# One five-bank place for the scores of both softmax maps, three single banks for the rest, and the order of the attention written anew

## The chip, the core and the metric

The kernel runs on one core of a Trainium2 chip. TensorE (PE) multiplies matrices into PSUM, which has eight banks of 512 fp32 columns on 128 partitions; VectorE (DVE) and ScalarE (ACT) read PSUM and SBUF, GpSimd (POOL) reads SBUF alone, and SyncE (SP) issues the DMAs. Each engine works through its own list in order and waits on semaphores for the others. The metric is the time of one launch in microseconds; the median of three runs of the kernel before is 1440.42 us (1439.58 to 1440.72).

## The reference

Two layers over 1024 latent tokens and 128 prompt tokens, width 1024. Each layer normalizes and modulates the tokens (adaLN), projects them into q, k, v, gates and the inputs of two local branches, mixes by attention, Fourier and gMLP, projects back and normalizes. The part that the change touches is the differential attention: each of four heads has two maps of 64 dimensions, each with a softmax of its own, and the second is subtracted.

```python
def _diff_attention(q, k, v, lam, subln_w, lam_init):
    s = jnp.einsum('bhqmd,bhkmd->bhmqk', q, k,
                   preferred_element_type=jnp.float32) * (HEAD_DIM ** -0.5)
    p = jax.nn.softmax(s, axis=-1)
    a = p[:, :, 0] - lam * p[:, :, 1]
    o = jnp.einsum('bhqk,bhke->bhqe', a, v.astype(jnp.float32))
    o = (o * lax.rsqrt(jnp.mean(jnp.square(o), axis=-1, keepdims=True) + RMS_EPS)
         * subln_w.astype(jnp.float32) * (1.0 - lam_init))
    return o.astype(v.dtype)
```

The latent tokens attend to 1152 keys (1024 latent, rotated, and 128 cached); the prompt tokens attend to their own 128.

## The kernel before

All matmuls that carry precision are done with a number split in a high and a low part: `f32r` high parts, and the remainder as a second operand.

**Attention.** `attention` (L695) runs over 4 heads of 8 blocks of 128 queries, in each of the two layers: 64 blocks. A block's steps are: for each map m, `score` (L632) makes 128x1152 scores in a three-bank tile S by two passes of three 384-column matmuls (high q against K, then the remainder `qlo` padded with zeros to 128 rows); DVE takes the row maximum (`nm`, L640) and ACT the exponential with its row sum (`P`, L642). `softmax_diff` (L580) scales and subtracts the maps (POOL L584, DVE L585). One block later `transpose` (L646) turns the difference by nine transposes into one three-bank tile T, which ACT copies (L655) and DVE takes the remainder of (L656). For each two blocks, `values` (L658) multiplies with V in 27 matmuls into `pv`, and `finish_o` (L592) normalizes by a matmul with a constant matrix and a row of small ACT, POOL and DVE steps.

**PSUM before.** `psS` (L78) has two places of three banks; S, T, pv and the rest go through them in turn. `psM` (L81) has two single banks for projections (`z`, `zt`), V's transposes (`vt`) and the prompt's steps (`sp`, `atp`, `pvp`).

**Order.** PE's order is written by hand (`manual_schedule`, L1059): after each step `attention` yields, and `fill.fill` puts so much projection work (in nominal ns, `FILL` times `SHARE`) behind it. `fill.until` forces the units that a head needs before it starts. A second stream, `extra`, makes the modulation of the next layer (`mods`, L177: DVE multiply-adds named `macc`, then four matmuls `mres`) from head `MHEAD` on. A third, `side`, takes one step of the prompt's attention (`prompt`, L670) at a time. The other engines' order is made by a scheduler that goes by emission order with priorities.

After attention come the gMLP and Fourier branches (`local_gmlp`, `fourier_prepare`, `local_fourier`) and the output projection (`out_proj`), whose last steps make the next layer's input (`make_h`).

## Time and profile before

| | |
|---|---|
| profiled execution | 1439.59 us, of which the span from first to last instruction is 1437.7 us |
| PE | 1330.9 us busy (93%), 8264 matmuls |
| PE's weight loads | 1236.6 us (86%), beside the matmuls |
| DVE, ACT, POOL | 907.6 (63%), 746.6 (52%), 793.4 us (55%) |
| TensorE clock granted | 0.979 of full on the mean |
| DMA | 114.43 MB, mean 80 GB/s |

PE is busy almost throughout, and its records overlap: a matmul's row lasts from its start until its result is out, while the next one has started. The time that a matmul takes from the engine is the distance between two starts, which is got from a run of many. Idle time of PE, and what ended it, is in the list of waits; the profiled times of the first and last block's maxima place layer 0's attention at 97.7 to about 600 us and layer 1's at 808.4 to about 1275 us.

### The profile page before, as it was taken

The page shows a single profiled execution, that of the slowest core. Times are in us where ns is not written, and L with a number is a line of the kernel's source. Part 1 is how long each engine was busy: PE and PEld are TensorE (multiplying, and loading weights), DVE is VectorE, ACT ScalarE, POOL GpSimd, SP SyncE. Part 2 cuts the span into 40 slices and gives each one's busy share as a digit, 9 for nine tenths or more (in the row PEclk, how much of TensorE's full clock was granted, in tenths as well). Part 3 has the DMA queues.
Part 4 walks back from the last instruction along what each step waited for, and adds up shares of the span by engine and source line. Part 5 has one row for each costly group of instructions (what it writes and reads, how often), then busy time and mean ns, then how long its engine had stood idle before and what let it go on. Part 6 is the DMA issues. An engine that isn't in the chain of part 4 may idle for free. (4 is left out here: it accounts for less than half of the span.)

```text
span 1437.7 us, 21298 instructions
## 1 busy us (share of the span) xinstructions
PE 1330.9 (93%) x8264; PEld 1236.6 (86%) x8264; DVE 907.6 (63%) x1354; ACT 746.6 (52%) x1380; POOL 793.4 (55%) x723
## 2 busy tenths in 40 slices
PE   6899998889899999999997989989799999999997
PEld 4689998879788998987887989988789999998786
DVE  3646667787877865355785565668775684435576
ACT  3576666557454444353656565755565544435320
POOL 2455657567563446336687676575575343533752
PEclk9999999999999999999999999999999999999999
DMA  9310102211220221363341100112020010126432
GB/s 337 147 49 17 35 18 65 75 46 36 88 76 22 98 74 42 108 211 114 124 161 45 50 19 32 49 44 80 32 65 3 30 47 30 47 78 221 154 133 80
DMA packets 56158, 114.43 MB, mean 80 GB/s; under 512 B 4973, under 2 KB 32493, under 8 KB 55929
## 3 DMA queue, kind: packets, MB, share of 16 engines
q1 hardware_dynamic: 56056, 113.07, 23.7%
q8 instruction: 65, 1.06, 0.3%
q14 instruction: 37, 0.30, 0.1%
HBM read 95.47 MB, written 17.58 MB: 79 GB/s over the span
## 5 line engine op out<-in xcount | busy, mean ns | idle before, releaser
L386 PE MATMUL z<-H,w 128*128 128x384 f32 x2520 | 499.8, 345 | 22.4 <-DVE V L506 5.0
L386 PEld LDWEIGHTS z<-H,w 128*128 128x128 f32 x2520 | 444.9, 193 | 29.0 <-ACT vT L492 4.9
L642 ACT ACTIVATE P<-S,nm 128x1152 f32<-128x1152 f32 x128 | 156.4, 1222 | 118.6 <-DVE nm L640 112.1
L640 DVE TENSOR_REDUCE nm<-S 128x1 f32<-128x1152 f32 x128 | 172.3, 1349 | 40.4 <-PE S L638 39.9
L401 PE MATMUL zt<-whi,H 128*128 128x256 f32 x1152 | 158.7, 285 | 4.8 <-ACT ug L767 3.4
L401 PEld LDWEIGHTS zt<-whi,H 128*128 128x128 f32 x1152 | 147.0, 192 | 7.5 <-ACT ug L767 4.0
L584 POOL TENSOR_SCALAR P<-P,rz,neglam 128x1152 f32<-128x1152 f32 x64 | 86.8, 1356 | 98.3 <-DVE rz L583 87.2
L585 DVE SCALAR_TENSOR_TENSOR P<-P,rz 128x1152 f32<-128x1152 f32 x64 | 105.2, 1643 | 42.3 <-POOL P L584 42.3
L630 POOL TENSOR_TENSOR qlo<-qr,Q 64x128 fp32r<-64x128 f32 x128 | 81.4, 641 | 86.8 <-PE S L638 80.2
L367 POOL TENSOR_TENSOR w<-wraw,w 128x1024 fp32r<-128x1024 f32 x36 | 89.6, 2489 | 65.4 <-ACT w L366 64.9
L638 PE MATMUL S<-K,Q 128*128 128x384 f32 x384 | 93.2, 351 | 21.4 <-DVE a L656 11.0
L662 PE MATMUL pv<-a,V 128*128 128x256 f32 x864 | 109.2, 283 | 3.1 <-ACT P L642 3.1
L662 PEld LDWEIGHTS pv<-a,V 128*128 128x128 f32 x864 | 106.6, 191 | 5.1 <-ACT P L642 5.1
L656 DVE TENSOR_TENSOR a<-T,a 128x1152 fp32r<-128x1152 f32 x64 | 86.6, 1353 | 37.5 <-ACT a L655 37.4
L638 PEld LDWEIGHTS S<-K,Q 128*128 128x128 f32 x384 | 67.6, 194 | 29.8 <-DVE a L656 12.8
L638 PE MATMUL S<-K,qlo 128*128 128x384 f32 x384 | 89.7, 342 | 0.0
L1013 PE MATMUL y<-wob,mx 128*128 128x512 f32 (+1 forms) x342 | 88.3, 385 | 1.5 <-DVE rr L1015 1.5
L655 ACT ACTIVATE a<-T 128x1152 fp32r<-128x1152 f32 x64 | 72.3, 1130 | 28.5 <-PE T L652 28.2
L406 PE MATMUL zt<-wlo,H 128*128 128x256 f32 x576 | 82.7, 284 | 1.1 <-POOL wlo L367 1.1
L1013 PE MATMUL y<-wo,mx 128*128 128x512 f32 (+1 forms) x342 | 81.6, 382 | 0.0
L652 PE MATMUL T<-cs,P 128*128 128x128 f32 x576 | 73.9, 274 | 3.8 <-ACT P L642 3.7
L406 PEld LDWEIGHTS zt<-wlo,H 128*128 128x128 f32 x576 | 74.9, 191 | 1.5 <-POOL wlo L367 1.5
(222 smaller groups left out, 2376.9 us busy)
## 6 DMA issues: line engine op xcount, KB each, us to landing
wraw<-in_w_in_dram SPq DMA_DIRECT2D x52, 512.0 KB, 3.3
wada<-in_w_ada_dram SPq DMA_DIRECT2D x32, 512.0 KB, 3.6
wa<-in_w_ada_dram SPq DMA_DIRECT2D x8, 1024.0 KB, 13.0
woraw<-in_w_out_dram SPq DMA_DIRECT2D x16, 512.0 KB, 3.9
mr<-mix SPq DMA_DIRECT2D x18, 384.0 KB, 3.2
mix<-gs SPq DMA_DIRECT2D x8, 576.0 KB, 3.9
x<-rr SPq DMA_DIRECT2D x9, 512.0 KB, 3.6
xr<-x SPq DMA_DIRECT2D x9, 512.0 KB, 5.3
```

Source lines behind the costliest of these rows:

```text
L367: eng.tensor_tensor(lo, raw, f(hi), op=ALU.subtract)
L386: pe.matmul(z, lhsT=w[:, a, kt, :], rhs=Hc[c][:, b, kt, :], start=n == 0, stop=n == 23)
L401: pe.matmul(z[:, i, :], lhsT=Hc[c][:, a, kt, o:o + 128], rhs=w[0][:, kt, :], start=n == 0, stop=False)
L406: pe.matmul(z[:, i, :], lhsT=Hc[c][:, 0, kt, o:o + 128], rhs=w[1][:, kt, :], start=False, stop=kt == KT - 1)
L584: pool.tensor_scalar(p2, p2, rz[:, 1:2], neglam[:, l:l + 1], op0=ALU.mult, op1=ALU.mult)
L585: return dve.scalar_tensor_tensor(p1, p1, rz[:, 0:1], p2, op0=ALU.mult, op1=ALU.add)
L638: pe.matmul(S[:, n, :CH], lhsT=q, rhs=K[:, m, n * CH:(n + 1) * CH], start=e == 0, stop=e == 1)
L640: dve.tensor_reduce(nm, S[:, :, :CH], axis=AX.XY, op=ALU.max, negate=True)
L642: act.activation(P.rearrange("p (c k) -> p c k", c=3), S[:, :, :CH], AF.Exp, bias=nm, accum_out=zz[:, m:m + 1])
L656: dve.tensor_tensor(lo, T[:, :, 0:3], f(hi), op=ALU.subtract)
L662: pe.matmul(pv[:, 0, :], lhsT=self.V[:, a, kt, :], rhs=self.A[:, b, kt, :], start=kt == 0 and e == 0, stop=kt == 8 and e == 2)
L1013: pe.matmul(z, lhsT=mx[:, a, k, :], rhs=wo[kt][b][:, ns], start=i == 0, stop=i == 23)
```

## The change

S becomes one tile of five banks (`psS`, one buffer): map 0 in columns 0 to 1151, map 1 in 1152 to 2303, 256 columns spare. All else, T and pv among them, goes through three single banks (`psM`). Both maps' first passes come one after the other in pieces that end at bank borders, then the remainders' pass. For it `pack` makes the remainder of q for both maps in one 128-row tile (`Q[:, 2]`: map 0 in rows 0 to 63, map 1 in rows 64 to 127), and five matmuls of 64 rows each run in alternate halves of the rows; the piece of map 0 that shares a bank with map 1 is made by a sixth, of 128 rows, against `kz`, the cached keys with zeros below. Transposes come in three thirds with projection work between, `values` directly after the last third of its second block, and the four prompt steps at a block's scores, in the spare columns. `GAPS` and `SCALE` set the projection work, evenly over heads 0 to 2 and more in head 3; `extra` goes by the same numbers.

```diff
-PACE = 2
-SHARE = [0.75, 1.25, 1, 1]
+GAPS = {True: (2600, 1300, 1300, 1900, 200), False: (2600, 1300, 1300, 1000, 0)}
-MFILL = 450
+MFILL = 0.42
-FILL = [1600, 1500, 1500, 2950]
+SCALE = [0.95, 0.95, 0.95, 1.4]
...
-    def psS(shape=(128, 3, 512), name="S"):
-        return ps.tile(list(shape), F32, name=name, tag="S", bufs=2)
+    def psS(shape=(128, 5 * 512), name="S"):
+        return ps.tile(list(shape), F32, name=name, tag="S", bufs=1)
...
-        return ps.tile(list(shape), F32, name=name, tag="mm", bufs=2)
+        return ps.tile(list(shape), F32, name=name, tag="mm", bufs=3)
...
+            kz = kzs[self.h % 2]
+            act.activation(kz[0:64], kc[0:64], AF.Copy)
...
+            for m in range(2):
+                r = slice(64 * m, 64 * m + 64)
+                pool.tensor_tensor(Q[r, 2], qr[r, qs], f(Q[r, m]), op=ALU.subtract)
...
+        def scores(self, Q, i, zz, aside):
+            S, K = psS(), self.K
+            ql = slice((i % 2) * 128, (i % 2) * 128 + 128)
+            parts = [[(0, 512), (512, 1024), (1024, 1152)], [(0, 384), (384, 896), (896, 1152)]]
+            for m in range(2):
+                for k0, k1 in parts[m]:
+                    pe.matmul(S[:, m * TOK + k0:m * TOK + k1], lhsT=Q[:, m, ql], rhs=K[:, m, k0:k1],
+                              start=(m, k0) != (1, 0), stop=False, skip_group_check=True)
+            pe.matmul(S[:, SEQ_S:TOK], lhsT=Q[:, 2, ql], rhs=self.kz, start=False, stop=True, skip_group_check=True)
+            for m, n in ((0, 0), (1, 1), (0, 1), (1, 2), (1, 0)):
+                r = slice(64 * m, 64 * m + 64)
+                k0, k1 = parts[m][n]
+                pe.matmul(S[:, m * TOK + k0:m * TOK + k1], lhsT=Q[r, 2, ql], rhs=K[r, m, k0:k1],
+                          start=False, stop=True, skip_group_check=True)
+            after = aside(S[:, 2 * TOK:]) if aside else None
...
+                dve.tensor_reduce(nm, Sm, axis=AX.X, op=ALU.max, negate=True)
+                P = tP(name="P")
+                act.activation(P, Sm, AF.Exp, bias=nm, accum_out=zz[:, m:m + 1])
...
-            T = psS((128, 3, 4, 128), "T")
+            T = psM((128, 3, 128), "T")
...
-            pv = psS((128, 2, 256), "pv")
+            pv = psM((128, 2, 256), "pv")
...
+                for c in range(3):
+                    with tc.high_priority(offset=EARLY):
+                        th.transpose(ti, ta, c)
+                    yield h, gaps[1 + c]
...
+            for h, ns in attention(l, fill):
+                fill.fill(ns * SCALE[h])
                 if h >= MHEAD:
-                    extra.fill(MFILL)
+                    extra.fill(ns * MFILL)
```

Smaller places follow the new tiles: `make_h` and the start's transposes take banks of the one S tile, and `mres`, `sg`, `pw` and `dftp` go to the single banks.

What the lists of the engines hold now, at three places. First PE, layer 0, head 1, third block of the kernel before: scores of map 0, projection (`z`), scores of map 1, projection, the nine transposes.

```order
L638 MATMUL S<-K,Q 128x384 [waits Activation_49]
L638 MATMUL S<-K,Q 128x384 x2
L638 MATMUL S<-K,qlo_104 128x384 [waits Pool_49]
L638 MATMUL S<-K,qlo_104 128x384 x2
L386 MATMUL z<-H_485,w_1681 128x384 x6
L638 MATMUL S<-K,Q 128x384 [waits DVE_49]
L638 MATMUL S<-K,Q 128x384 x2
L638 MATMUL S<-K,qlo_104 128x384 [waits Pool_49]
L638 MATMUL S<-K,qlo_104 128x384 x2
L386 MATMUL z<-H_121,w_1859 128x384 x12
L652 MATMUL T<-cs,P 128x128 [waits PE_49,Activation_49]
L652 MATMUL T<-cs,P 128x128 x8
```

The scores of a block in the same head now, both maps in one piece; the first row is the wait for the one S tile.

```order
L640 MATMUL S<-K,Q 128x512 [waits Activation_49]
L640 MATMUL S<-K,Q 128x512
L640 MATMUL S<-K,Q 128x128
L640 MATMUL S<-K,Q 128x384
L640 MATMUL S<-K,Q 128x512
L640 MATMUL S<-K,Q 128x256
L643 MATMUL S<-kz_107,Q 128x128 [waits Pool_49]
L647 MATMUL S<-K,Q 128x512 x3
L647 MATMUL S<-K,Q 128x256
L647 MATMUL S<-K,Q 128x384
```

Twelve matmuls of 384 columns became twelve of other widths, the last five with 64 rows. Second, PE in the block before that one (the second of the head) from its first third of the transposes to its end.

```order
L669 MATMUL T<-cs,P 128x128 [waits Activation_49]
L669 MATMUL T<-cs,P 128x128 x2
L386 MATMUL z<-H_480,w_1629 128x384 x9
L669 MATMUL T<-cs,P 128x128 [waits DVE_49]
L669 MATMUL T<-cs,P 128x128 x2
L386 MATMUL z<-H_480,w_1629 128x384 x3
L386 MATMUL z<-H_119,w_1873 128x384 [waits DVE_49]
L386 MATMUL z<-H_119,w_1873 128x384 x2
L669 MATMUL T<-cs,P 128x128 [waits DVE_49]
L669 MATMUL T<-cs,P 128x128 x2
L386 MATMUL z<-H_119,w_1873 128x384 x6
```

Between this block's scores and these rows stand the pv normalization and 15 `z`; each third waits for a bank and has projection work behind it. Third, DVE in a block of head 1 before, from the maximum of map 0.

```order
L640 TENSOR_REDUCE nm<-S 128x1 [waits PE_49]
L679 TENSOR_REDUCE nmp<-sp 128x1 [waits PE_49]
L640 TENSOR_REDUCE nm<-S 128x1 [waits PE_49]
L604 SCALAR_TENSOR_TENSOR gs<-msq,gs 128x256 [waits Pool_49]
L583 RECIPROCAL rz<-zzp 128x2 [waits Activation_49]
```

And DVE in the second block of head 1 now.

```order
L654 TENSOR_REDUCE nm<-S 128x1 [waits PE_49]
L654 TENSOR_REDUCE nm<-S 128x1 [waits Activation_49]
L672 TENSOR_TENSOR a<-T,a 128x3x128 [waits DVE_49,Activation_49]
L417 TENSOR_TENSOR gs<-z,gt 128x384 [waits Activation_49]
L583 RECIPROCAL rz<-zz_1941 128x2 [waits Activation_49]
L672 TENSOR_TENSOR a<-T,a 128x3x128 [waits Activation_49]
L607 SCALAR_TENSOR_TENSOR gs<-msq,gs 128x256 [waits Pool_49]
L585 SCALAR_TENSOR_TENSOR P<-P,rz 128x1152 [waits Pool_49]
L672 TENSOR_TENSOR a<-T,a 128x3x128 [waits Activation_49]
L417 TENSOR_TENSOR gs<-z,gt 128x384 [waits Activation_49]
```

The second maximum waited for PE and now waits for ACT, in all 64 blocks; in 38 of them it stands directly behind the first.

## Rows read from the trace of the kernel before

**Rows 1.** The page's head and PE's busy time.

```profile
span 1437.7 us, 21298 instructions
...
PE 1330.9 (93%) x8264; PEld 1236.6 (86%) x8264; DVE 907.6 (63%) x1354; ACT 746.6 (52%) x1380; POOL 793.4 (55%) x723
```

**Rows 2.** Windows: both attention stretches, head 1; length, busy (count) by engine, clock, DMA.

```profile
97.70:600.00 502.30, 468.27 (x3079) 446.28 (x3078) 345.26 (x469) 271.07 (x499) 286.84 (x261) 0.98 0.18 58
808.40:1275.00 466.60, 439.32 (x2971) 425.55 (x2970) 300.87 (x431) 260.41 (x485) 260.47 (x253) 0.99 0.13 43
193.10:299.10 106.00, 97.53 (x607) 94.41 (x605) 78.31 (x88) 63.62 (x121) 68.81 (x67) 0.98 0.19 59
```

**Rows 3.** PE's waits: total us, times, longest.

```profile
PE S L638 <- DVE a L656: 11.0, 3, 4.8
...
PE atp L685 <- DVE rz L583: 6.4, 4, 2.3
PE S L638 <- ACT P L642: 5.2, 4, 1.8
PE S L638 <- ACT msq L598: 5.0, 3, 2.4
...
PE T L652 <- ACT P L642: 3.7, 2, 1.9
...
PE z L386 <- ACT Pp L687: 2.9, 2, 1.5
...
PE z L386 <- ACT Pp L680: 2.8, 4, 1.2
...
PE atp L685 <- ACT P L642: 2.0, 2, 1.0
```

**Rows 4.** Chain of waits: start, us, what, matmuls in it.

```profile
1100.07 3.23 PE pv L662 x27
...
1149.87 1.04 PE S L638 x6
...
1315.97 8.19 PE dft L923 x36
```

**Rows 5.** Timeline of PE, layer 1, head 2: start, length, line, shape, count.

```profile
1104.70 0.59 PE L594 MATMUL pv<-sq,cs 128*128 128x256 f32 x2
1105.13 1.15 PE L652 MATMUL T<-cs,P 128*128 128x128 f32 x9
1106.03 7.01 PE L386 MATMUL z<-H,w 128*128 128x384 f32 x39
1112.88 0.33 PE L638 MATMUL S<-K,Q 128*128 128x384 f32 x1
```

**Rows 6.** Timeline of PE around matmuls with 32 of the array's columns each.

```profile
34.10 0.47 PE L333 MATMUL modt<-h,modacc 128*128 128x2 f32 x3
34.50 1.07 PE L327 MATMUL macc<-wa,h 128*32 128x256 f32 x16
35.50 0.44 PE L305 MATMUL z<-H,w 128*128 128x384 f32 x1
```

**Rows 7.** Groups by line: busy us, mean ns, idle before.

```profile
L640 DVE TENSOR_REDUCE nm<-S 128x1 f32<-128x1152 f32 x128 | 172.3, 1349 | 40.4 <-PE S L638 39.9
L585 DVE SCALAR_TENSOR_TENSOR P<-P,rz 128x1152 f32<-128x1152 f32 x64 | 105.2, 1643 | 42.3 <-POOL P L584 42.3
L656 DVE TENSOR_TENSOR a<-T,a 128x1152 fp32r<-128x1152 f32 x64 | 86.6, 1353 | 37.5 <-ACT a L655 37.4
L506 DVE TENSOR_TENSOR V<-vt,V 128x384 fp32r<-128x384 f32 (+1 forms) x24 | 12.1, 506 | 12.5 <-ACT V L502 7.8 <-ACT vp L504 4.7
L642 ACT ACTIVATE P<-S,nm 128x1152 f32<-128x1152 f32 x128 | 156.4, 1222 | 118.6 <-DVE nm L640 112.1 <-DVE P L585 5.7
L642 ACT ACTIVATION_READ_ACCUMULATOR P<-S,nm 128x1 f32 x128 | 24.7, 193 | 0.0
```

**Rows 8.** Timeline: DVE's second maximum beside ACT's first exponential, head 1.

```profile
203.05 1.35 DVE L640 TENSOR_REDUCE nm<-S 128x1 f32<-128x1152 f32 x1
...
203.44 1.22 ACT L642 ACTIVATE P<-S,nm 128x1152 f32<-128x1152 f32 x1
```

More of the change, by code (lines that the diff above doesn't have):

```diff
@@ L192, in mods @@
         ba = mods_bias(l, part)
-        mres = psS((2, 2, 512), "mres")
         for n in range(2):
+            ns = slice(n * 512, (n + 1) * 512)
+            mres = psM((2, 512), "mres")
             for c in range(2):
-                pe.matmul(mres[:, n], lhsT=sel2[:, c], rhs=acc[c][:, n * 512:(n + 1) * 512], start=c == 0, stop=c == 1)
-        mods_finish(l, part, [mres[:, n] for n in range(2)], ba)
+                pe.matmul(mres, lhsT=sel2[:, c], rhs=acc[c][:, ns], start=c == 0, stop=c == 1)
+            dve.tensor_tensor(ba[:, ns], mres, ba[:, ns], op=ALU.add)
+            yield 1000
+        mods_finish(l, part, ba)
         yield 1000
@@ new lines, in scores, with after @@
+            def scores(free):
+                S = [psM((128, 128), "sp"), free[:, 0:128]]
+                for m in range(2):
+                    r = slice(64 * m, 64 * m + 64)
+                    pe.matmul(S[m], lhsT=self.qp[r], rhs=self.kp[r], start=True, stop=True)
+                def after():
+                    nm = small([128, 2], "nmp", 2)
+                    zz = small([128, 2], "zzp", 2)
+                    for m in range(2):
+                        dve.tensor_reduce(nm[:, m:m + 1], S[m], axis=AX.X, op=ALU.max, negate=True)
+                        act.activation(P[:, m], S[m], AF.Exp, bias=nm[:, m:m + 1], accum_out=zz[:, m:m + 1])
+                    softmax_diff(self.l, P[:, 0], P[:, 1], zz, "p")
+                return after
@@ L695, in attention @@
+            return [scores, turn, product, norm]
     def attention(l, fill):
@@ L698, in attention @@
         turn = None
-        done = None
-        side = Stream()
-        for n in range(8 * H + 2):
+        finish = None
+        side = []
+        for n in range(8 * H + 1):
             h, i = min(n // 8, H - 1), n % 8
+            gaps = GAPS[i % 2 == 0]
             if n < 8 * H:
@@ L712, in attention @@
                 with tc.high_priority(offset=EARLY):
-                    p1 = hd.score(Q, i, 0, zz)
-                if i < 7:
-                    hd.low(i + 1, Qn)
-                with tc.high_priority(offset=EARLY):
-                    side.fill(1)
-                yield h, 0
-                with tc.high_priority(offset=EARLY):
-                    p2 = hd.score(Q, i, 1, zz)
+                    p1, p2 = hd.scores(Q, i, zz, side.pop(0) if side else None)
                 if i % 2 == 0 and i < 6:
@@ L744, in attention @@
+            if n < 8 * H:
+                yield h, gaps[0]
             if turn:
                 th, ti, ta = turn
-                with tc.high_priority(offset=EARLY):
-                    th.transpose(ti, ta)
+                for c in range(3):
+                    with tc.high_priority(offset=EARLY):
+                        th.transpose(ti, ta, c)
+                    yield h, gaps[1 + c]
                 if ti % 2 == 1:
-                    done = th, ti // 2
+                    if ti == 1:
+                        fill.until((l, U_G + th.h))
+                        th.begin_values()
+                        side += th.prompt()
+                    with tc.high_priority(offset=EARLY):
+                        finish = th.values(ti // 2), th if ti == 7 else None
+                    yield h, gaps[4]
@@ L750, in attention @@
                 turn = None
-                with tc.high_priority(offset=EARLY):
-                    side.fill(1)
-                yield h, 3
             if n < 8 * H:
```

169 lines of the change are left out of this document (69 added, 100 removed).

## The prediction

> **What bounds the kernel now.** I read the page first, then windows, then PE's waits, then single rows for prices. The page says that PE is busy for 93% of a span of 1437.7 us [rows 1]; the profiled execution took 1439.59 us, 1.9 more than its span and 0.8 below the median of 1440.42, so a sum against it holds for the median too. The two attention stretches fill 968.9 us of the span. In them PE is idle for 502.3 - 468.3 = 34.0 and 466.6 - 439.3 = 27.3 us, 61.3 together, and the granted clock of 0.98 and 0.99 loses about 0.02 x 502 + 0.01 x 467 = 15 us more [rows 2]. All else there is matmul time. A change to attention can thus gain from three stocks: the matmul time itself, those 61 us of idleness, and the 15 us of clock that hang on them. DVE is the next in line: 78 of 106 us in head 1 [rows 2], in order, with every step of the softmax in its list.
>
> The reader is to see in the waits that 21.2 us of the idle time come before scores (11.0 + 5.2 + 5.0), 14.1 around the prompt's steps (6.4 + 2.9 + 2.8 + 2.0) and 3.7 before transposes [rows 3]: 39 us at places that the change rebuilds.
>
> **Prices of a matmul.** A 384-column matmul takes 0.175 us (39 start between 1106.03 and 1112.88) and a transpose 0.10 (nine between 1105.13 and 1106.03) [rows 5]; 256 columns take 0.120 (27 in 3.23) and 512 take 0.227 (36 in 8.19) [rows 4].
>
> **The scores.** Before, a block's scores are two runs of six matmuls, 2 x 1.04 = 2.09 us [rows 4]. Now the first pass is three of 512, one of 384, one of 256 and one of 128: 0.681 + 0.175 + 0.120 + 0.10 = 1.08 us. The piece against `kz` is 0.10. The last five, with 64 rows each, would take 3 x 0.227 + 0.175 + 0.120 = 0.98 us one after the other. If the halves of the array run side by side, the upper half works 2 x 0.227 = 0.45 and the lower 0.227 + 0.120 + 0.175 = 0.52.
>
> No row shows halves of rows, but the nearest show quarters of columns: sixteen matmuls of 256 columns start within 1.00 us, 34.50 to 35.50 [rows 6], where two of the same width with all columns need 0.43, 1104.70 to 1105.13 [rows 5]. Four times four, at 0.215 a round, make 0.86: the quarters do run together, and about 0.14 is left for the way back to the full array. The way in cost some 0.07: the three `modt` ahead of them each last 0.25, so the last began at 34.32, the next was due at 34.43 and came at 34.50 [rows 6]. I take 0.21 for one change to halves and back. For the low pass the bounds are 0.52 and 0.98; I take 0.61, the overlapped value with one weight load of 0.1 (a transpose's distance) that nothing covers, since it is nearest to the quarters' row. A block is then 1.08 + 0.10 + 0.61 + 0.21 = 2.0 us, 0.1 less than before, and 64 blocks gain **6 us**. By the bounds it is from -11 (0.52) to +18 us (0.98).
>
> The Trainium skill, in "TensorE: Matmul & The Clock Gate", Part 3, says that a weight load overlaps a running matmul only when its row group differs (the background buffer is named beside it). By that alone the second and third matmul of a half would load in the open and the low pass would take about 0.9; the sum would be +13 instead of -6. The macc rows speak against it: their sixteen share all rows and yet lose nothing between rounds.
>
> **The one S tile.** This is the part that can hurt. Before, the maximum of map 1 runs beside the exponential of map 0 (203.05 to 204.40 against 203.44) [rows 8]. Now DVE's list shows it waiting for ACT, in every block, and 38 times nothing stands between. The chain of a block is scores 2.0, maximum 1.35, exponential and row sum 1.22 + 0.19, maximum 1.35, exponential 1.41 [rows 7], and about 0.3 for four handovers (an estimate): 7.85 us until the next block's scores may start. PE's own work between two starts in an odd block of heads 0 to 2 is 2.0 + 36 x 0.175 + nine transposes 0.9 + the constant-matrix matmul 0.43 = 9.6 us [rows 5]; in an even one 42 of the 384-column matmuls and pv make it 13.5. So the scores are covered by 1.75 us in odd blocks and by over 5 in even ones and in head 3. Behind a maximum that is held stand, in DVE's list, the remainder of T's first third, a gate's product and the reciprocal; for T's third PE waits two thirds later, when its bank is wanted.
>
> How much of the 1.75 is eaten by other work in the two lists? DVE's work in such a block is 2 x 1.35 + 1.41 held + 1.64 + 3 x 0.51 = 7.3 us [rows 7] before gates, rotations and finishing, 76% of 9.6. Before, a block without pv is 27 matmuls of 384, two scores and nine transposes, 7.7 us, and DVE's part 2 x 1.35 + 1.64 + 1.35 = 5.7, 74%. DVE's list is no lighter, but the chain has more room. I put the new waits at half a microsecond in each of the 24 odd blocks of heads 0 to 2: **12 us**; the bounds are 0 and, for a delay of 4 us, 24 x 2.25 = 54.
>
> **Thirds, pv, prompt.** Three evictions of 0.51 replace one of 1.35 on DVE [rows 7]: 64 x 0.18 = 11 us more DVE work, beside PE. A third's bank is wanted again some 2.9 us later, after a filling of nine, the next third and a filling of six; its eviction takes ACT's copy, DVE's 0.51 and their queues, and DVE's list puts the last third behind the 1.64 of the map subtraction. pv starts only some 2 us after the last third, and its last nine matmuls need it. I put 8 us there, with bounds of 0 and 64 x 0.5 = 32. The prompt's steps now stand at a block's scores with a whole block for what comes between two of them; their 14.1 us go. So do the 21.2 before scores and the 3.7 before transposes. The other waits (projections' banks, V) I leave as they are. Idle time: -39 + 12 + 8 = **-19 us**. [...]
>
> **What costs nothing.** The copy for `kz`, the halved number of remainder steps on POOL and the spread of macc lie beside PE; uncovered, macc would show as a wait at `mres`, where the order gives it a full block. The start and the local branches use the same number of banks or more, under 2 us either way.
>
> Sum: 1439.6 - 6 - 19 - 3 = 1411.6; I say **1411 us**.
>
> **Rivals.** (1) *The single S tile decides.* In odd blocks DVE's and ACT's lists delay the chain by 4 us; 1.75 are covered, so 24 blocks wait 2.25 each, +54 in place of +12, and T and pv queue behind held maxima, +24 in place of +8. The idle sum becomes -39 + 54 + 24 = +39, the clock +5: 1439.6 - 6 + 39 + 5 = 1478. It decides from a delay of 1.75 us on; at 3 us (+30, +16, clock 0) it gives 1441. For it: 38 direct holds, and 76% of DVE's time in fixed work. Against it: half of the blocks have 5 us of room. Chance 0.2; its middle is 1460.
> (2) *The halves of rows don't overlap*: +18 in place of -6, 1436; chance 0.08. Or they overlap, but each half waits for its own next weights: 0.1 us before the second and the third matmul of a half, a low pass of 0.9, +13 in place of -6, 1431; chance 0.04. For both: no row shows row halves. Against: the quarters. The second is what the page named above would have.
> (3) *The idle time only moves*, from S and the prompt to the three single banks, where T, pv, z and V now meet: 1439.6 - 6 = 1434. For it: DVE's load stays. Against: evenly spaced fillings. Chance 0.18.
> My forecast has 0.5, with its own range 1390 to 1428.
>
> **Chances.** What a measurement of this kernel can tell from no change is about 0.2%, 3 us. The forecast is all faster (0.5). Of (2) and (3), 0.30 together, with some 10 us around 1435, 0.17 are faster, 0.06 within, 0.07 slower. Of (1), 0.16 are slower, 0.02 within and 0.02 faster. That makes 0.69, 0.08 and 0.23. The range is 1378 to 1450: below it all stocks would have to pay at once (-11, -39, -10), above it lies half of (1).
>
> **What would show it.** Scores: the five 64-row matmuls start in overlapping pairs, and a block's scores last about 2.0 us; at 2.3 or more (2) holds. S: the wait of PE's first score for ACT's exponential, in odd blocks, about 12 us in all; over 40 is (1). Prompt: no wait on `rz` or `Pp` is left for PE. Thirds: waits of T, pv and z together below 30 us. DVE: idle before the second maximum about 1.4 us in most blocks, named as ACT's P. The forecast is wrong if PE's idle time in attention is above 50 us, or if its matmul time changed by more than the bounds.

## The result, and where the time went

The changed kernel takes 1508.21 us (median, 1505.15 to 1509.83) against 1440.00 for the kernel before in the same comparison: 1.047 times as long (95% interval 1.045 to 1.049). The forecast, 1411 within 1378 to 1450, was wrong in sign and size.

The page of the changed kernel, against [rows 1]: engine, busy us, share of the span, instructions.

```profile
span 1508.0 us, 21422 instructions
...
PE 1351.0 (90%) x8264; PEld 1208.2 (80%) x8264; DVE 924.5 (61%) x1482; ACT 749.4 (50%) x1508; POOL 770.7 (51%) x657
```

The span grew by 70.3 us. PE's idle time is span minus busy: 106.8 before, 157.0 now, **+50.2**. Its busy time grew by 20.1, of which the clock makes **13.5**: the mean granted clock fell from 0.979 to 0.971, and 0.029 x 1508 - 0.021 x 1437.7 is 13.5. The remaining 6.6 us are in its rows. Of the 50.2, 39.5 stand in the two attention stretches below, 4.0 at the start, 5.8 between the stretches and 0.9 at the end. So this is first a story of waits, and then of the clock.

The two attention stretches, against [rows 2] (length, busy us of PE, PEld, DVE, ACT, POOL; then clock, DMA share, GB/s):

```profile
106.70:640.00 533.30, 477.64 (x3127) 434.46 (x3126) 354.60 (x543) 276.20 (x569) 268.48 (x229) 0.98 0.18 55
850.20:1345.00 494.80, 449.70 (x2965) 414.19 (x2965) 303.17 (x495) 261.39 (x547) 245.47 (x218) 0.97 0.13 39
```

PE is idle for 55.7 and 45.1 us there, 100.8 in place of 61.3; the forecast called itself wrong above 50. What PE waits for, against [rows 3]: what it was about to do, what ended the wait, us in total, times, longest.

```profile
PE T L669 <- DVE a L672: 21.5, 27, 2.6
PE S L640 <- ACT P L656: 10.7, 2, 5.4
PE T L669 <- DVE V L506: 10.6, 8, 4.1
PE pv L684 <- DVE gs L595: 8.1, 4, 2.8
...
PE z L386 <- DVE a L672: 7.0, 3, 2.5
...
PE S L713 <- DVE Pp L585: 6.3, 4, 2.5
...
PE T L669 <- DVE P L585: 4.0, 4, 1.6
PE T L669 <- ACT zz L424: 3.6, 4, 1.3
...
PE T L669 <- DVE gmg L417: 2.7, 2, 1.4
...
PE T L669 <- DVE gs L417: 1.9, 3, 0.9
PE T L669 <- ACT msq L601: 1.8, 2, 0.9
PE T L669 <- ACT Pp L708: 1.8, 2, 0.9
```

Before, transposes waited 3.7 us, for the exponential that still read their place [rows 3]. Now they wait 49.5, and only the 4.0 of `DVE P L585` are for their source. The others name the last reader of another tile of the single banks: an earlier third (`a`), V's transposes (`V`), a projection (`zz`, `gmg`, `gs`), pv (`msq`), the prompt's score (`Pp`): 43.9 us, by the releasers that the profile infers. The groups show it once more, with DVE's idle time (busy us, mean ns of one, idle before and what ended it):

```profile
L654 DVE TENSOR_REDUCE nm<-S 128x1 f32<-128x1152 f32 x128 | 173.2, 1353 | 114.0 <-ACT P L656 76.8 <-PE S L647 17.0 <-PE S L718 10.3
...
L669 PE MATMUL T<-cs,P 128*128 128x128 f32 x576 | 100.0, 283 | 49.5 <-DVE a L672 21.5 <-DVE V L506 10.6 <-DVE P L585 4.0
L672 DVE TENSOR_TENSOR a<-T,a 128x384 fp32r<-128x384 f32 x192 | 104.3, 549 | 41.8 <-ACT a L671 41.2
...
L684 PE MATMUL pv<-sq,cs 128*128 128x256 f32 x64 | 21.5, 417 | 8.1 <-DVE gs L595 8.1
```

The last row is the ones-matmul that normalizes pv. In the kernel before PE never waited there:

```profile
L594 PE MATMUL pv<-sq,cs 128*128 128x256 f32 x64 | 19.1, 379 | 0.0
```

There DVE's `gs` product, which reads the same bank, was issued behind the ones-matmul; the change issues it ahead, right after pv (`begin_o`). By the releaser these 8.1 us come from that order, not from the number of banks.

How such a wait comes about, in layer 0, head 1 (timeline of three engines: start, length, instruction, and in brackets idle before and what ended it):

```profile
256.94 0.55 PE L669 MATMUL T<-cs,P 128*128 128x128 f32 x3 [0.89 <-ACT Pp L708]
257.14 1.22 ACT L656 ACTIVATE P<-S,nm 128x1152 f32<-128x1152 f32 x1
...
257.24 1.30 PE L386 MATMUL z<-H,w 128*128 128x384 f32 x6
...
258.49 1.36 DVE L654 TENSOR_REDUCE nm<-S 128x1 f32<-128x1152 f32 x1 [3.47 <-ACT P L656]
258.64 0.49 ACT L671 ACTIVATE a<-T 128x384 fp32r<-128x384 f32 x1
...
259.32 0.50 ACT L424 ACTIVATE zz<-z 128x384 f32<-128x384 f32 x1
...
259.76 0.55 DVE L672 TENSOR_TENSOR a<-T,a 128x384 fp32r<-128x384 f32 x1
...
259.88 0.55 PE L669 MATMUL T<-cs,P 128*128 128x128 f32 x3 [1.33 <-ACT zz L424]
```

The first third is done at 257.49. Its copy starts at 258.64, behind the exponential of the block just scored and a step of pv's normalization, its remainder at 259.76, behind the second maximum, and its bank is free at 260.31, 2.8 us after the transposes. The next third needs a bank in the meantime and gets that of a projection, copied out at 259.82, and starts 0.06 us later.

The scores themselves came out as forecast (timeline of PE):

```profile
235.15 1.26 PE L640 MATMUL S<-K,Q 128*128 128x512 f32 x6
236.25 0.22 PE L643 MATMUL S<-kz,Q 128*128 128x128 f32 x1
236.40 0.79 PE L647 MATMUL S<-K,Q 64*128 64x512 f32 x5
237.12 2.70 PE L386 MATMUL z<-H,w 128*128 128x384 f32 x14
```

From the first 64-row matmul to the next full one are 0.72 us, less than the 0.98 that the forecast reckons for five in a row. A block takes 1.98, the median of the 64.

### The profile page after: what moved, and what is told of

The parts are those of the page before. It is cut to its first block, busy times and chain, and to the rows that moved or that the text cites. A ratio compares the mean times of both kernels' runs of the same rounds, so it can differ in the third digit from the quotient of the medians.

```text
span 1508.0 us, 21422 instructions
## 1 busy us (share of the span) xinstructions
PE 1351.0 (90%) x8264; PEld 1208.2 (80%) x8264; DVE 924.5 (61%) x1482; ACT 749.4 (50%) x1508; POOL 770.7 (51%) x657
## 4 chain that ended last, share of the span: by engine, by line
PE 43%; DVE 20%; ACT 12%; DMA 9%; POOL 8%; issue 5%; SPq 2%; DVEq 0%; POOLq 0%; ACTq 0%
PE z L386 10%; PE y L1035 9%; PE zt L401 6%; PE pv L678 5%; DVE nm L654 4%; ACT P L656 4%; DVE macc L188 3%; PE S L640 3%; PE zt L406 3%; DMA wada<-in_w_ada_dram 3%; DMA woraw<-in_w_out_dram 3%; DVE P L585 2%; PE S L647 2%; PE T L669 2%; DVE a L672 2%
## 5 line engine op out<-in xcount | busy, mean ns | idle before, releaser
L386 PE MATMUL z<-H,w 128*128 128x384 f32 x2520 | 521.8, 354 | 18.8 <-DVE a L672 7.0
L386 PEld LDWEIGHTS z<-H,w 128*128 128x128 f32 x2520 | 446.6, 195 | 31.9 <-DVE a L672 10.2
L654 DVE TENSOR_REDUCE nm<-S 128x1 f32<-128x1152 f32 x128 | 173.2, 1353 | 114.0 <-ACT P L656 76.8
L669 PE MATMUL T<-cs,P 128*128 128x128 f32 x576 | 100.0, 283 | 49.5 <-DVE a L672 21.5
L672 DVE TENSOR_TENSOR a<-T,a 128x384 fp32r<-128x384 f32 x192 | 104.3, 549 | 41.8 <-ACT a L671 41.2
L669 PEld LDWEIGHTS T<-cs,P 128*128 128x128 f32 x576 | 68.3, 143 | 76.2 <-DVE a L672 25.2
L585 DVE SCALAR_TENSOR_TENSOR P<-P,rz 128x1152 f32<-128x1152 f32 x64 | 109.9, 1717 | 18.6 <-POOL P L584 18.3
L671 ACT ACTIVATE a<-T 128x384 fp32r<-128x384 f32 x192 | 93.2, 490 | 55.5 <-PE T L669 55.3
L640 PE MATMUL S<-K,Q 128*128 128x512 f32 (+3 forms) x384 | 84.9, 358 | 11.0 <-ACT P L656 10.7
L406 PE MATMUL zt<-wlo,H 128*128 128x256 f32 x576 | 87.5, 289 | 2.6 <-DVE wlo L367 1.7
L628 POOL TENSOR_TENSOR Q<-qr,Q 64x256 fp32r<-64x256 f32 x64 | 52.3, 818 | 60.0 <-ACT Q L622 55.1
L1035 PEld LDWEIGHTS y<-wob,mx 128*128 128x128 f32 x342 | 61.8, 189 | 22.1 <-DVE rr L1037 8.4
```

The source lines that it names most:

```text
L386: pe.matmul(z, lhsT=w[:, a, kt, :], rhs=Hc[c][:, b, kt, :], start=n == 0, stop=n == 23)
L406: pe.matmul(z[:, i, :], lhsT=Hc[c][:, 0, kt, o:o + 128], rhs=w[1][:, kt, :], start=False, stop=kt == KT - 1)
L585: return dve.scalar_tensor_tensor(p1, p1, rz[:, 0:1], p2, op0=ALU.mult, op1=ALU.add)
L640: pe.matmul(S[:, m * TOK + k0:m * TOK + k1], lhsT=Q[:, m, ql], rhs=K[:, m, k0:k1], start=(m, k0) != (1, 0), stop=False, skip_group_check=True)
L654: dve.tensor_reduce(nm, Sm, axis=AX.X, op=ALU.max, negate=True)
L669: pe.transpose(T[:, kt, :], a[:, (3 * c + kt) * 128:(3 * c + kt + 1) * 128], ident)
```

## The experiments

All but the last group edit the changed kernel, as "after" here; the others the kernel before. Idle is span minus PE's busy time of the profiled execution; T is PE's idle time before the transposes of the attention tile, from the group of their line.

| kernel | base | us (median) | times before (95%) | idle | clock | T |
|---|---|---|---|---|---|---|
| before | | 1440.0 | 1 | 106.8 | 0.979 | 3.8 |
| after | | 1508.2 | 1.045-1.049 | 157.0 | 0.971 | 49.5 |
| e6 two single banks | after | 1774.3 | 1.228-1.234 | 338.5 | 0.927 | 132.1 |
| e5 thirds closer, later | after | 1554.4 | 1.074-1.080 | 183.9 | 0.952 | 80.0 |
| e17 thirds apart, earlier | after | 1524.2 | 1.057-1.062 | 167.8 | 0.967 | 51.6 |
| e1 both maxima first | after | 1541.1 | 1.070-1.074 | 178.1 | 0.961 | 70.9 |
| e7 six banks, two singles | after | 1776.5 | 1.230-1.236 | 335.6 | 0.924 | 146.7 |
| e9 copy out first | after | 1533.8 | 1.062-1.067 | 168.6 | 0.959 | 55.4 |
| e18 both pieces on DVE | after | 1525.8 | 1.058-1.063 | 168.2 | 0.964 | 62.6 |
| e10 ones ahead of scores | after | 1513.3 | 1.048-1.054 | 150.0 | 0.958 | 43.8 |
| e13 T in the wide place | after | 1559.1 | 1.080-1.085 | 191.3 | 0.955 | 31.3 |
| e4 less fill | after | 1555.7 | 1.080-1.085 | 181.8 | 0.958 | 55.7 |
| e8 more fill | after | 1516.6 | 1.051-1.056 | 163.2 | 0.969 | 56.8 |
| e2 start's banks | after | 1513.2 | 1.050-1.054 | 157.6 | 0.964 | 53.2 |
| e14 prompt alone | before | 1453.9 | 1.008-1.012 | 118.2 | 0.977 | 23.1 |
| e19 joint scores | before | 1463.5 | 1.014-1.020 | 124.7 | 0.976 | 1.8 |
| e3 joint, halves | before | 1500.8 | 1.040-1.045 | 144.9 | 0.963 | 16.4 |
| e16 joint, halves, slack | before | 1484.2 | 1.029-1.034 | 143.8 | 0.976 | 20.1 |
| e12 copy out first | before | 1474.4 | 1.021-1.026 | 128.3 | 0.969 | 14.1 |
| e20 3% other fill | before | 1457.6 | 1.010-1.014 | 121.8 | 0.979 | 12.5 |

None beats the kernel before.

**One single bank fewer (e6).**

```diff
-        return ps.tile(list(shape), F32, name=name, tag="mm", bufs=3)
+        return ps.tile(list(shape), F32, name=name, tag="mm", bufs=2)
...
-                        side += th.prompt()
+                        side += [None] + th.prompt()
```

> 

> Edit to the changed kernel: two single banks instead of three (the wide place stays at five; the eighth bank is unused), and the prompt's steps begin one block later, so that no three of the small tiles are open at once. Theory B (the banks decide): with one bank less the waits before T and z rise by 40 us or more, time 1550 and up. Theory E (the queues of ScalarE and VectorE decide, banks are free when they have passed): waits rise by less than 15 us, time 1508-1525.

PE's groups of this kernel:

```profile
L386 PE MATMUL z<-H,w 128*128 128x384 f32 x2520 | 558.2, 370 | 69.8 <-DVE a L672 21.6 <-ACT zz L424 20.5 <-ACT msq L601 5.0
...
L669 PE MATMUL T<-cs,P 128*128 128x128 f32 x576 | 112.5, 310 | 132.1 <-ACT msq L601 39.7 <-DVE a L672 26.2 <-DVE gs L417 23.4
```

266 us more: waits before T and z went from 68 to 202 us, far beyond theory B's 40. With thirds, pv and projections in the single banks, one bank fewer is dear. What a fourth would give back is not shown: five and three banks are all that there are.

**Thirds closer (e5) and further apart (e17).**

```diff
-GAPS = {True: (2600, 1300, 1300, 1900, 200), False: (2600, 1300, 1300, 1000, 0)}
+GAPS = {True: (4200, 1000, 1000, 1000, 100), False: (4200, 1000, 1000, 0, 0)}   # e5
+GAPS = {True: (1400, 1900, 1900, 1900, 200), False: (1400, 1900, 1900, 1000, 0)}   # e17
```

> 

> Edit to the changed kernel: the same fill per block, but 4200 instead of 2600 units of it ahead of the first third of the transposes, and 1000 instead of 1300 between thirds. Theory E (the burst): the thirds come due while ScalarE and VectorE run the two exponentials and the second maximum of the block just scored (145 exponentials stood ahead of 192 copies of thirds); 1.5 us later they find free queues, PE's waits before transposes fall from 49 us to under 25 and the time to 1475-1492. Theory B (three banks): thirds that follow each other faster wait more for banks, and pv for the last remainder; waits before T and pv stay above 60 us, time 1508-1525.

> 

> Edit to the changed kernel: the thirds further apart (1900 units of fill between them for 1300), the first one 1200 earlier, the same sum. At 1000 units between them the time was 1554, with waits before T of 80 us; at 1300 1508 and 49. Theory B (a third wants a bank that the tile three before still holds): at 1900 the waits before T fall to 25-35 and the time to 1485-1498. Theory E (queues): the first third now meets the first exponential, waits stay, 1508-1525.

The row of the transposes in e5, then in e17:

```profile
L669 PE MATMUL T<-cs,P 128*128 128x128 f32 x576 | 104.4, 294 | 80.0 <-DVE a L672 51.4 <-ACT zz L424 11.5 <-DVE V L506 7.4
```

```profile
L669 PE MATMUL T<-cs,P 128*128 128x128 f32 x576 | 100.0, 284 | 51.6 <-DVE a L672 16.6 <-DVE P L585 12.2 <-ACT zz L424 6.0
```

Closer is worse by 46 us, and the wait for an earlier third goes from 21.5 to 51.4, against theory E; pv, which follows closer too, waits 10.2 for 4.6. Further apart takes 4.9 off the wait for an earlier third, but the first third, earlier by 1200, now waits for its source (`P`, 12.2 in place of 4.0). It is 16 us slower: theory B's figure missed, theory E's (waits stay, 1508 to 1525) met.

**The held maximum (e1, e7).**

```diff
             for m in range(2):
-                nm = small([128, 1], "nm", 4)
-                Sm = S[:, m * TOK:(m + 1) * TOK]
-                dve.tensor_reduce(nm, Sm, axis=AX.X, op=ALU.max, negate=True)
+                dve.tensor_reduce(nms[m], Ss[m], axis=AX.X, op=ALU.max, negate=True)
+            for m in range(2):
                 P = tP(name="P")
-                act.activation(P, Sm, AF.Exp, bias=nm, accum_out=zz[:, m:m + 1])
+                act.activation(P, Ss[m], AF.Exp, bias=nms[m], accum_out=zz[:, m:m + 1])
```

> 

> Edit to the changed kernel: both row maxima are issued before both exponentials, so that the second maximum stands directly behind the first in VectorE's list and the first exponential waits for it instead. Theory A (the held maximum): in the changed kernel VectorE stood 76.8 us before second maxima, and the remainders of the transposes behind them came late; with the stand gone PE's waits before transposes fall from 48 us to under 25, and the time to 1465-1490. Theory B (three single banks): thirds, pv, z and V want each other's banks whatever the maximum does; PE's waits before transposes stay above 35 us and the time within 8 us of 1508. Against A as well: the first exponential is now 1.35 us later, and what waits for it on ScalarE.

Groups of e1:

```profile
L654 DVE TENSOR_REDUCE nm<-S 128x1 f32<-128x1152 f32 x128 | 167.7, 1350 | 42.8 <-PE S L647 18.7 <-PE S L714 9.0 <-PE S L719 7.8
...
L670 PE MATMUL T<-cs,P 128*128 128x128 f32 x576 | 102.9, 290 | 70.9 <-DVE a L673 36.4 <-ACT msq L601 8.3 <-DVE gs L417 7.9
```

DVE's 76.8 us behind ACT are gone, as built, and the kernel is 33 us slower; neither range had that. The two exponentials now stand in one run ahead of ACT's copies: a first third is copied 1.7 us after its transposes instead of 0.8, though its remainder then follows after 0.39 instead of 0.67 (means of 64). So this way of removing the hold does not pay; what the hold costs alone, e1 does not tell. In the example above the held maximum stands ahead of the remainder. Over the whole trace of the changed kernel that is a small part: a held maximum still runs at the end of the copy in 29 of 192 thirds, and takes 15.5 of the 145.8 us between copies and remainders.

e7 gives each map three banks of a six-bank place, and the single banks are two; the low pass becomes three pairs without the padded piece, and both of the prompt's score tiles go into the place:

```diff
-    def psS(shape=(128, 5 * 512), name="S"):
+    def psS(shape=(128, 6 * 512), name="S"):
...
+            M = 3 * 512
...
-                Sm = S[:, m * TOK:(m + 1) * TOK]
+                Sm = S[:, m * M:m * M + TOK]
```

> 

> Edit to the changed kernel: the wide place has six banks, three per map, so that no bank holds columns of both maps, two single banks are left, the low pass is three pairs of 64 rows without the zero-padded piece, and both of the prompt's score tiles lie in spare columns. To be held against the two-single-bank kernel of the same call, which differs in the shared bank. If the shared bank costs (the second maximum waits for the first exponential, 76.8 us of VectorE's time, and the second exponential comes 1.35 us later): 20-40 us faster than that kernel, idle time of VectorE before second maxima under 15 us. If the held maximum costs nothing in itself: within 8 us of it.

```profile
L648 DVE TENSOR_REDUCE nm<-S 128x1 f32<-128x1152 f32 x128 | 173.6, 1356 | 154.6 <-ACT P L650 87.4 <-PE S L641 28.8 <-PE S L707 11.6
```

The time is that of e6, but the hold did not go (87.4 us): in all 64 blocks the second maximum starts behind the first exponential though no bank is shared. The order came with the place, not with the bank, and e7 leaves the price of the hold untested.

**Emptying a bank sooner (e9, e18, e10).**

```diff
-            act.activation(hi, T, AF.Copy)                      # e9
-            dve.tensor_tensor(lo, T, f(hi), op=ALU.subtract)
+            act.activation(ac, T, AF.Copy)                      # ac: the third's columns of a
+            act.activation(hi, ac, AF.Copy)
+            dve.tensor_tensor(lo, ac, f(hi), op=ALU.subtract)
...
-            act.activation(hi, T, AF.Copy)                      # e18
+            dve.tensor_copy(hi, T)
...
-GAPS = {True: (2600, 1300, 1300, 1900, 200),                    # e10, and finish[0]() ahead of hd.scores
+GAPS = {True: (2600, 1300, 1300, 900, 1200),
```

> 

> Edit to the changed kernel: ScalarE first copies a third from its bank to SBUF (over the columns of the attention tile that the transposes have just read), and both pieces are then made from there. A bank is held for one copy instead of a copy and a remainder: from the last transpose 1.1 us instead of 2.42 (0.62 + 0.49 + 0.76 + 0.55, means over 192 thirds). Theory B (how long the three banks are held decides): PE's waits before T fall from 49 us to 20-28, time 1470-1490. Rival: ScalarE gets 192 x 0.4 = 80 us more work and the exponentials come later; 1508-1530.

> 

> Edit to the changed kernel: VectorE makes both pieces of a third, ScalarE none (94 us of ScalarE's work go, some 100 us come to VectorE). With 81 us more on ScalarE (copy out first) the time rose by 26, though the banks were free sooner. Theory H (what an eviction waits for is the exponentials ahead of it in ScalarE's list): waits before T fall below 35, 1480-1498. Theory I (VectorE is the fuller list, 61% of the span, and the held second maximum stands in it): waits rise, 1525-1560.

> 

> Edit to the changed kernel: the normalising ones-matmul of pv stands ahead of the next block's scores instead of behind them, with 1200 of the 1900 units of fill before pv moved between pv and it. Its bank was held 9.6 us on average (from pv's first matmul to ScalarE's read of the mean square, which queued behind the next exponentials); now about 6. Theory B: waits before T and z fall by 10-15 us, time 1485-1500. Rival: pv now waits for the last third's remainder, since only 900 units lie between; within 6 us of 1508 or slower.

PE's waits in e9:

```profile
PE T L669 <- DVE V L506: 14.7, 5, 4.2
PE T L669 <- ACT P L672: 13.8, 13, 5.0
PE T L669 <- DVE P L585: 12.8, 10, 2.5
PE pv L686 <- DVE gs L595: 12.6, 8, 3.9
```

DVE's remainder in e9, which reads SBUF alone:

```profile
L674 DVE TENSOR_TENSOR a<-P,a 128x384 fp32r<-128x384 f32 x192 | 160.5, 845 | 38.7 <-ACT a L673 38.0
```

In e9 the wait for an earlier third (now for its copy, `P L672`) fell from 21.5 to 13.8, as B has it, but the waits for the source, V and `gs` rose. Not ACT alone got more work (81 us, 830.7 busy): a remainder takes DVE 845 ns instead of 549, 56 us in all, and POOL is busy for 817.9 us instead of 770.7. Which of the three lists makes the 26 us was not separated, so e9 is no clean test of emptying sooner. e18 took ACT's copies away, and DVE's additions cost 18 us: theory H falls, theory I has the waits (62.6) and, at its edge, the time. e10 is 5 us slower, as its rival has it (pv waits 9.6 us). In its profiled execution, which is 5 us above its median, idle time is 7 less than in the changed kernel, the clock lower (0.958), and the ones-matmul waits 13.2 us for DVE's `gs`. Which way of emptying the banks would be cheap was not found.

**Transposes back in the wide place (e13).** The nine go into the score place after its second exponential; pv stands behind the next scores.

```diff
-            T = psM((128, 3, 128), "T")
+            T = S[:, 0:1536].rearrange("p (c k q) -> p c k q", c=3, k=4)
...
-GAPS = {True: (2600, 1300, 1300, 1900, 200), False: (2600, 1300, 1300, 1000, 0)}
+GAPS = {True: (0, 5600, 3000), False: (900, 1400, 3000)}
...
-SCALE = [0.95, 0.95, 0.95, 1.4]
+SCALE = [0.93, 0.93, 0.93, 1.36]
```

> 

> Edit to the changed kernel: the nine transposes go, as a whole, into the wide place itself once both exponentials have read it, and are moved out by one copy and one remainder before the next scores; pv is issued behind the next block's scores (3.2 us that cover the softmax chain), and fill amounts are set for that order. The single banks then serve z, pv and V alone. Joint scores, row halves, the held maximum and the prompt's place stay as in the changed kernel. Theory B (thirds in the single banks are the loss): PE's waits before T go below 15 us, those before scores rise to 15-30 for the remainder, time 1420-1455. Theory F (issuing both maps together is the loss wherever the transposes go, as the kernel with the old places and joint scores suggests): 1490-1515.

```profile
L641 PE MATMUL S<-K,Q 128*128 128x512 f32 (+3 forms) x384 | 89.5, 370 | 43.3 <-DVE a L674 37.4 <-ACT P L657 5.5
...
L670 PE MATMUL S<-cs,P 128*128 128x128 f32 x576 | 82.5, 293 | 31.3 <-DVE gs L595 18.1 <-ACT Pp L710 6.8 <-ACT P L657 6.2
...
L686 PE MATMUL pv<-sq,cs 128*128 128x256 f32 x64 | 26.8, 507 | 56.2 <-DVE gs L595 56.1
```

z waits for no third any more, but the kernel is 51 us slower: the ones-matmul waits 56.1 us for DVE's `gs`, issued ahead of it as in the changed kernel and in 21 of 32 cases directly behind a maximum, and scores wait 37.4 for the transposes' remainder. The first of these I put down to the order that I gave it (900 units ahead of the ones seem too few), which no run changes. So e13 does not decide on theory B: the waits on the single banks' tenants went, and larger ones took their place. Both ranges were passed.

**Fill and start (e4, e8, e2).**

```diff
-SCALE = [0.95, 0.95, 0.95, 1.4]
+SCALE = [0.83, 0.78, 0.78, 1.53]     # e4
+SCALE = [1.0, 1.0, 1.0, 1.25]        # e8
...
-        if c and kp % 2 == 0:          # e2
+        if kp % 2 == (0 if c else 1):
```

> 

> Edit to the changed kernel: the fill amounts per block are scaled to the totals that the kernel before had (11.9 and 11.2 us of weight per pair of blocks in heads 0-2 in place of 12.8, more in head 3). Theory D (only displaced work: heads 0-2 took in 14 us per layer more of the projections): heads 0-2 shorten by some 13 us per layer, head 3 lengthens by less, time 1495-1505. Theory A: a shorter fill uncovers the chain from scores to scores, waits of the scores for the exponential rise from 10.7 us to 20-35, time 1508-1525.

> 

> Edit to the changed kernel: 5% more projection work per block in heads 0-2 (scale 1.0 for 0.95), less in head 3 (1.25 for 1.4). With less fill the kernel was 48 us slower. If the blocks' length is set by the softmax chain and not by PE's work, more fill is free in heads 0-2 and PE's waits fall by 10-20 us: 1488-1500. Rival: the optimum lies near 0.95 because head 3 runs out of fill; then 1505-1520.

> 

> Edit to the changed kernel: in the start, the transposes of the first token chunk take single banks for every second pair instead of always the same two spare banks of the wide place. Theory C (the reused banks): the first score maximum comes back from 106.7 us to 98-100 and the time falls by about 7, to 1501. Rival: the start's 9 us are the clock, which fell at 70.0 and 93.9 us for reasons of its own; then the time stays within 3 us of 1508.

Less fill costs 48 us, more costs 8: of the three sets of amounts the changed kernel's is the best, and no sign is left that a wrong amount makes the 68 us. e2 moved the first maximum from 106.7 to 107.8 instead of 98, and is 5 us slower: theory C falls. Of the start's 9 us the windows give 4 as idle time (23.6 of 106.7 against 19.6 of 97.7) and 3.5 as clock (0.94 against 0.97); its two falls are at 58.7 and 82.6 us of the span.

**Parts in the kernel before (e14, e19, e3, e16, e12) and a control (e20).** e19 keeps the full-array low pass; e12 is e9's edit, for the nine transposes at once.

```diff
+            after = aside(S[:, 0, CH:512]) if aside else None      # e14: prompt steps at the scores
...
-                    p1 = hd.score(Q, i, 0, zz)                     # e19, e3, e16: both maps at once
+                    p1, p2 = hd.scores(Q, i, zz)
...
+            for n in range(3):                                     # e3, e16: low pass in row halves
+                for m in range(2):
+                    r = slice(64 * m, 64 * m + 64)
+                    pe.matmul(Ss[m][:, n, :CH], lhsT=Q[r, 2, ql], rhs=K[r, m, n * CH:(n + 1) * CH], start=False, stop=True)
...
-SHARE = [0.75, 1.25, 1, 1]                                         # e16
+SHARE = [0.75, 0.75, 0.5, 2]
-FILL = [1600, 1500, 1500, 2950]
+FILL = [1700, 1680, 1680, 2550]                                    # e16
+FILL = [1640, 1540, 1540, 2850]                                    # e20, nothing else
```

> 

> Edit to the kernel before: only the prompt's part of the change. Its steps are issued at the scores, one per block (the two score products at the two maps of one block), and write the 128 spare columns of the score place in use instead of single banks. By the forecast the prompt's waits (8.4 us before its transposes, some of the 17.5 before z, whose banks they shared) go: 1424-1432. Rival: the waits move into the scores, as the changed kernel's 6.3 us before the prompt's turn did, and a score place is held longer by the prompt's own softmax: 1440-1455.

> 

> Edit to the kernel before: both maps' scores are issued one directly after the other, with the full-array low pass as before (2.09 us a block); places, prompt, fill amounts as before. Theory G (the joint issue is the loss): the time is that of the joint kernel with row halves, 1500.75, plus what the halves gained, 64 x 0.3 = 19 at most: 1500-1520. Rival (the row halves are the loss, through the array's divisions): 1438-1450.

> 

> Edit to the kernel before: two places of three banks, single banks, fill amounts and prompt as before, but a block's scores for both maps are issued together, and the low pass is three pairs of 64-row matmuls. By the measured pairs of the changed kernel (4 ns apart) a block's scores are 6 x 0.175 + 3 x 0.175 + 0.2 = 1.8 us instead of 2.09, 64 blocks gain 19 us. Theory A and B alike (the loss is in the one wide place or the three single banks, not in the row halves): 1415-1430. Rival: issuing both maps together is itself the loss, since transposes and pv then find both wide places taken until the exponentials are done; then 1440-1470.

> 

> Edit to the kernel before with joint scores and row halves (1500.75 us): fill moved from ahead of the transposes to behind them (shares 0.75, 0.75, 0.5, 2 for 0.75, 1.25, 1, 1) and 12% more fill in heads 0-2, so that the transposes' place, asked back by the next joint scores, has 3.4 us for its copy and remainder instead of 1.5. Theory G (joint scores take the slack of the transposes' place): waits of the scores fall from 45 us to under 20, time 1455-1475, and the gain of the halves begins to show. Rival: pv and the transposes, now earlier, wait for the exponentials that hold their places instead; 1495 and up.

> 

> Edit to the kernel before: ScalarE copies the nine transposes out of their wide place at once, and both pieces are made from SBUF; the place is free after one copy (1.13 us) instead of copy and remainder with their queues (1.13 + 0.86 + 1.35). If places are what scores wait for there too (11.0 us on a remainder), these waits go below 4 us and the time to 1428-1436. Rival: 64 x 1.1 = 70 us more of ScalarE's work delays exponentials and rotations; 1440-1455.

> 

> Edit to the kernel before: fill amounts 1640, 1540, 1540, 2850 instead of 1600, 1500, 1500, 2950, nothing else. If a step of 14 us (the prompt's part alone) means something, this moves the time by less than 5 us: 1435-1445. If the kernel sits on a point that any re-timing leaves, it costs 8-20 us: 1448-1460.

PE's groups in e14, e19, e3, e16 and e20, in this order:

```profile
L656 PE MATMUL T<-cs,P 128*128 128x128 f32 x576 | 78.7, 285 | 23.1 <-ACT Pp L687 10.4 <-ACT P L644 7.4 <-DVE gs L702 5.2
```

```profile
L639 PE MATMUL S<-K,Q 128*128 128x384 f32 x384 | 95.3, 357 | 39.3 <-DVE a L660 30.5 <-ACT P L646 6.0 <-ACT msq L598 2.2
```

```profile
L633 PE MATMUL S<-K,Q 128*128 128x384 f32 x384 | 96.0, 371 | 46.0 <-DVE a L658 39.8 <-ACT msq L597 3.5 <-ACT P L643 1.9
...
L654 PE MATMUL T<-cs,P 128*128 128x128 f32 x576 | 76.7, 280 | 16.4 <-ACT P L643 16.4
```

```profile
L664 PE MATMUL pv<-a,V 128*128 128x256 f32 x864 | 112.3, 288 | 20.0 <-ACT P L643 20.0
...
L633 PE MATMUL S<-K,Q 128*128 128x384 f32 x384 | 80.9, 341 | 11.5 <-DVE a L658 5.8 <-ACT msq L597 2.7 <-ACT P L643 2.4
...
L654 PE MATMUL T<-cs,P 128*128 128x128 f32 x576 | 77.8, 283 | 20.1 <-ACT P L643 20.1
```

```profile
L386 PE MATMUL z<-H,w 128*128 128x384 f32 x2520 | 500.4, 345 | 30.0 <-ACT vT L492 12.9 <-ACT Pp L680 7.1 <-DVE gs L417 3.4
...
L652 PE MATMUL T<-cs,P 128*128 128x128 f32 x576 | 75.0, 276 | 12.5 <-ACT P L642 12.5
```

The **control** is the run to read the others by: 3% other fill costs 17 us. Its waits sit elsewhere (S 11.7 for 21.4, T 12.5 for 3.8, z 30.0 for 22.4), with 15 us more in all. The kernel before stands on a point that this nudge leaves; an edit that costs 14 or 17 there has shown no more than that. It is one nudge, and of the kernel before; what a nudge does to the changed kernel no run tells, so its steps of 5 to 18 us (e2, e8, e10, e17, e18) should be read with the same care.

**e14** (+14) says that the prompt's move brings none of its 14 us: 10.4 come back before T as `Pp`, and the prompt's own transposes wait 10.6 for 8.4. **e19** (+22.5) is 5 beyond the control and between its two ranges; its scores wait 30.5 us for the transposes' remainder [rows 3: 11.0], since both places are asked back at once. **e3** (+61) is well beyond, with 39.8 of the same wait. With room given back (**e16**) that wait falls to 5.8, as theory G has it, but 40 us of waits on exponentials stand before pv and T (16.4 in e3), and 44 us of loss stay. **e12** brings the scores' wait down to 1.7 us from 21.4 and loses 34: T, z and pv wait more. ACT has 63 us more there, a remainder takes DVE 1.60 us instead of 1.35, and POOL is busy 41 us longer. Why halves with joint scores lose 37 us more than joint scores alone isn't settled: of the 31.5 between the profiled spans 20 are idle time and about 20 clock, with some 9 of matmul time gained.

## Why the forecast was wrong

- **Scores: right.** 2.0 us forecast, 1.98 measured, overlapping pairs. The weight loads of the second pair start at 236.51, while the first pair runs in the same halves until 236.90. The Trainium skill's rule ("TensorE: Matmul & The Clock Gate", Part 3: only where the row group differs; weighed at +13) is not what this trace shows. The second pair starts 0.34 us after the first, where 512 columns take 0.227: that 0.11 is about the one uncovered load that the forecast put in.
- **S waits: size right, place wrong.** 10.7 us against 12, but in two waits of over 5 us in the second block of each layer, none in the odd blocks that the term was made of. That the sizes agree is luck.
- **Thirds and pv: the step that failed.** Forecast 8 us, bounds 0 and 32; measured 49.5 before T instead of 3.8, and 4.6 + 8.1 before pv and its ones instead of 3.1: **+55**. I wrote that a third's bank "is wanted again some 2.9 us later", and took that for the whole demand on it. From the last transpose a bank is empty after 2.42 us on the mean (0.62 until the copy, 0.49, 0.76 until the remainder, 0.55), so thirds alone would fit; but the bank has other tenants, a projection, V's transposes, pv and the prompt's score, and each waits its turn in DVE's or ACT's list. The 8.1 before the ones are another matter, the new place of `gs`, which the forecast did not price.
- **-39 us of stock gone: failed.** Scores, prompt and transposes were to lose their waits. The prompt's 8.4 before its transposes are gone, 6.3 wait inside the scores instead; S as a whole went from 21.4 to 17.3. e14 moves the prompt's waits alone and e12 removes the scores'; both times they return elsewhere.
- **Held maximum.** It stands 76.8 us, 1.2 per block, as forecast (1.4). Rival 1 had scores wait 54 us for it; they wait 10.7. It also had T and pv queue behind it. e1 and e7 do not price that; by the 15.5 us above it is a small part of what delays remainders.
- **Rival 3** (idle time moves to the three single banks, 1434) had the place, at no net cost, and was too cheap.
- **Clock: wrong sign.** The sum has -3, which no run shows; measured +13.5. In the large the clock is lower where idle time is longer (e6: 338.5 us, 0.927), but not in step: e10 has 7 us less of it than the changed kernel and 0.958, e20 15 more than the kernel before and 0.979. **Start**: "under 2 us", measured 9.
- **The bounds** ended where the single terms did. No term allowed for re-timing as such, which e20 puts at 17 us for a 3% nudge.

What is shown: the loss is waits (+50 us) and clock (+13.5); most of the waits are before transposes, on banks whose other tenants DVE and ACT empty late (43.9 of 49.5 us by the releasers); one bank fewer costs 266 us (e6), and denser thirds, later and with pv closer, 46 (e5). Tried without gain: other fill amounts (e4, e8), the start's banks (e2), another place of the ones (e10), no held maximum (e1). Argued, not shown: that banks emptied faster would give the time back. Two tries (e9, e18) each loaded DVE's or ACT's list, and lost there; no run gave any of the 68 us back. How much of them is re-timing as such, by a new order that was tried at only a few other points (e4, e5, e8, e10, e17), all slower, stays open.

## What to carry to other kernels

Waits in a kernel whose matmul engine is over 90% busy are not a stock that an edit can cash in: name for each what is late next, and price the tile's hold by all tenants of its banks and by the lists that empty them. Before reading a 1% step of an edit, nudge a constant by 3% and see what that alone does: of the eighteen edits here, eight came out slower than every range on record for them (e1, e2, e3, e4, e5, e9, e12, e13), whose ranges priced a mechanism and not the re-timing beside it. When two in-order engines empty the same small banks, relieving one by loading the other moves the wait, and can cost more than it saves.

## What was not expected of the hardware

64-row matmuls on different halves of the rows do run side by side: five of them with 256 to 512 columns pass in 0.72 us with the way back to the full array, where the distances of matmuls of full height add up to 0.98. A row's length is not what an instruction takes from the engine: the rows of nine transposes in a run last 1.15 us [rows 5] and those of three 0.55, but the next matmul starts 0.90 after the first of nine and 0.30 after the first of three (256.94 to 257.24), so cutting them in thirds costs PE nothing by itself. A remainder of 384 columns takes DVE 549 ns with one source in PSUM and 845 with both in SBUF (e9); for 1152 columns it is 1353 and 1599 (e12), and POOL's busy time grows by 47 and 41 us in these runs. A copy that frees a bank early costs the other engines as well as ScalarE: e9 lost 26 us and e12 34, and the runs do not divide that among the lists.
